# A decoder trunk in three-part float32 products: the order of seven products on PSUM accumulators, the place of a norm's scale, and the order of gates, tail and end of attention

## The chip, the cores and the metric

The kernel runs on one core of one Trainium2 chip. Its metric is the device time of one execution in microseconds (us). The engines are TensorE (PE in the profile), VectorE (DVE), ScalarE (ACT) and GpSimd (POOL); SyncE (SP) only issues transfers. Each engine works through its own list of instructions in order and waits for others by semaphores.

## What is computed

One layer of a decoder on 512 tokens of width 1024, in float32. x is the residual stream:

```
h = rmsnorm(x, g_mix);  proj = h @ w_in            # q, k, v of two attentions, two gates
y_a = stick_breaking_attention(...) @ w_up_a;  y_b = sliding_window_attention(...) @ w_up_b
x = x + (sigmoid(gate_a) * y_a + sigmoid(gate_b) * y_b) @ w_o
h = rmsnorm(x, g_mlp)
x = x + square(relu(h @ w_ff1)) @ w_ff2            # hidden width 4096
pe = p @ w_pe                                      # p: 512 x 256
x = x + pe * sigmoid(rmsnorm(x, g_pe) @ w_pg)
return rmsnorm(x, g_final)
```

rmsnorm multiplies by 1/sqrt(mean of squares + 1e-6) and by a weight g for each column.

## The kernel before

Each float32 operand of a product is split into a high part (a rounding to a shorter format, made by ACT) and a low part (the rest, made by DVE); `split` does this, and `mm3` makes three matrix products of the parts (high x high, low x high, high x low) on one PSUM bank. `unit` loads a block of 128 x 1024 weights by SP into a buffer wr and splits it into whi and wlo. PSUM has eight banks, named by tags: p (3), z (2), at (2), o (1).

The stages are: the first projections; sliding-window attention (`sliding`); values and, pair by pair of heads, `project` and `breaking` (stick-breaking attention, whose head h ends in a product `so` and whose pair ends in the operand oa, for the last pair oa3h and oa3l); gates ag and bg (`gates`, 24 matrix products each) and outputs ay and by (`outputs`, 12 each); merged gates times w_o (wo); the second norm and transposes to h2; the MLP; then the gate product pg, pe times its sigmoid, and the final norm.

The MLP's hidden columns are taken in four quarters q. A quarter has eight hidden blocks f (24 matrix products each, then relu and square into u). Its product with w_ff2 is done by a scheme of seven half-size products instead of eight (`products`): operands are sums and differences of quarters of u (s1, s2, s3, made by DVE) and of w_ff2. The sums of weights are made by transfers: SP loads a block into tx or t1, and POOL issues further loads that add to what is there. The seven products, p1 to p7, have 24 matrix products each and go to accumulators pa, pb, pc of two banks each; `onto` adds an accumulator to x2, the residual stream in SBUF. `products` is a generator; the loop over hidden blocks takes one step of the quarter before after each block, in the order p1, p7, p6, p2, p5, p4, p3, so that only the last quarter's seven stand without blocks between them. The first product is also kept in `both`, over all quarters, and added to three parts of x2 at the end.

The order within the engines is made by a scheduler from the order of the code, the free buffers and its own estimate; only the first stage has its ACT and DVE order by hand. In the second norm, r2 = 1/sqrt(mean + eps) is found by small DVE steps and x times r2 is written to xn; PE does `embed` (pe = p @ w_pe, both halves of 512 columns) meanwhile, then transposes xn. In the tail `injected` takes a bank of pg: sigmoid (ACT, L672), times pe and plus x2 (DVE, L673, L675), square with a sum over the row (ACT, L677), times g_final (POOL, L681). For each of the four row tiles t, `rsqrt` makes 1/sqrt by eight small steps (L119 to L130), both halves are scaled (L716 on DVE, L718 on ACT) and sent out (L719).

Of the kernel before, what the change touches and what calls it, by code (L numbers as in the profile page):

```python
# [17 lines left out]
P = 128  # L18
# [15 lines left out]
FOUR = ("p", "p", "z", "z")  # L34
# [8 lines left out]
def trunk(ctx, tc, xT_in, x_in, pT_in, w_in, w_up_a, w_up_b, w_o, w_ff1, w_ff2, w_pe, w_pg, g_final, pack, scratch, out):  # L43
# [12 lines left out]
    every = ["p", "p", "p", "z", "z", "at", "at", "o"]  # L56
# [371 lines left out]
    def gates(name, i):  # L428
        for m in (2 * i, 2 * i + 1):
            ps = bank(f"{name}g{m}")  # L430
            columns(ps, unit(w_in[(18 if name == "a" else 26) + m], P), h1)
            g = scaled(slot(f"{name}t{m}", "x" if name == "b" else "t"), ps, rb)
            nc.scalar.activation(g, g, AF.Sigmoid)
            gate[name, m] = g

    def outputs(name, i):
        w = unit((w_up_a if name == "a" else w_up_b)[i], 256)
        for j in range(2):
            m = 2 * i + j
            g = gate[name, m]  # L440
            ps = bank(f"{name}y{m}")
            columns(ps, w, oa if name == "a" else ob, j * P)
            nc.vector.tensor_tensor(g, g, ps, op=ALU.mult)
# [38 lines left out]
    def plain(name):  # L482
        return fpool.tile([P, U], F32, tag="raw", name=name, bufs=10)

    def factor(name):
        return [fpool.tile([P, U], F32R, tag=f"m{e}", name=f"m{e}{name}", bufs=3) for e in ("hi", "lo")]

    def half(name, tag, n):
        return fpool.tile([P, S], F32, tag=tag, name=name, bufs=n)
# [5 lines left out]
    phl = [b.rearrange("p (k c) -> p k c", k=2) for b in factor("pT")]  # L495
    split(*phl, pT)


    x2 = [[slot(f"x2_{t}{j}", "x") for j in range(2)] for t in range(NT)]
    ss = [small(f"ss2_{j}", 4) for j in range(2)]  # L500
    for j in range(2):
        for t in range(NT):
            nc.sync.dma_start(x2[t][j], x_in[t * P:(t + 1) * P, j * S:(j + 1) * S])
        ps = [bank(f"wo{j}_{t}", (FOUR, ("at", "at", "o", "p"))[j][t]) for t in range(NT)]
        for c in range(4):
            whi, wlo = unit(w_o[4 * j + c], S)
            for k in range(2):
                hi, lo = merged[2 * c + k]
                for t in range(NT):
                    cols = slice(t * P, (t + 1) * P)  # L510
                    mm3(ps[t], hi[:, cols], lo[:, cols], whi[:, k], wlo[:, k], c == 0 and k == 0, c == 3 and k == 1)
        for t in range(NT):
            nc.vector.tensor_tensor(x2[t][j], x2[t][j], ps[t], op=ALU.add)
            junk = half(f"junk{j}{t}", "e", 3)
            nc.scalar.activation(junk, x2[t][j], AF.Square, accum_out=ss[j][:, t:t + 1])
# [8 lines left out]
    pe = [[half(f"pe{t}{j}", "pe", 8) for j in range(2)] for t in range(NT)]  # L524

    def embed(j):
        whi, wlo = unit(w_pe[j], S)
        ps = [bank(f"pe{j}_{t}", ("p", "p", "z", "z" if j == 0 else "z")[t]) for t in range(NT)]
        for k in range(2):
            for t in range(NT):  # L530
                cols = slice(t * P, (t + 1) * P)
                mm3(ps[t], phl[0][:, k, cols], phl[1][:, k, cols], whi[:, k, :], wlo[:, k, :], k == 0, k == 1)
        for t in range(NT):
            nc.scalar.copy(pe[t][j], ps[t])

    embed(0)
    embed(1)

    h2 = [pair(f"h2_{k}", "h") for k in range(KD)]
    for k in range(KD):  # L540
        ps = bank(f"h2p{k}", every[k])
        for t in range(NT):
            nc.tensor.transpose(ps[:, t * P:(t + 1) * P], xn[t][:, k * P:(k + 1) * P], ident)
        split(*h2[k], ps, gcol(1, k))
# [3 lines left out]
    both = [half(f"both{t}", "e", 3) for t in range(2)]  # L548
    tt = nc.vector.tensor_tensor

    def products(q, ua, ub):
        a11, a21 = [ua[:, :, i * 256:(i + 1) * 256] for i in range(2)]
        a12, a22 = [ub[:, :, i * 256:(i + 1) * 256] for i in range(2)]
        b11, b21, b22, t1, tx = [[None] * 2 for _ in range(5)]

        def block(c, kh, jh):
            return w_ff2[((q * 2 + kh) * 2 + jh) * 2 + c]

        def load(name, c, kh, jh):
            b = plain(f"{name}_{q}{c}")  # L560
            nc.sync.dma_start(b, block(c, kh, jh))
            return b

        def more(t, kh, jh):
            for c in range(2):
                nc.gpsimd.dma_start(t[c], block(c, kh, jh), accum_op=ALU.add)  # L566

        for c in range(2):
            b11[c], tx[c], t1[c], b22[c] = load("b11", c, 0, 0), load("tx", c, 0, 1), load("t1", c, 0, 1), load("b22", c, 1, 1)
        more(tx, 1, 1)  # L570
        more(t1, 0, 0)

        def area(name, tags):
            return [bank(f"{name}{q}_{i}", tags[i]) for i in range(2)]

        def product(name, a, b, ps, start, stop, g=None):
            m = [x.rearrange("p (k c) -> p k c", k=4) for x in factor(f"{name}{q}")]
            split(*m, a, g)
            for c in range(2):
                count[0] += 1  # L580
                w = [wpool.tile([P, U], F32R, tag=f"w{e}", name=f"w{e}{count[0]}", bufs=3) for e in ("hi", "lo")]
                split(*w, b[c])
                whi, wlo = [x.rearrange("p (k c) -> p k c", k=2) for x in w]
                for k in range(2):
                    for i in range(2):
                        cols = slice(i * P, (i + 1) * P)
                        mm3(ps[i], m[0][:, 2 * c + k, cols], m[1][:, 2 * c + k, cols], whi[:, k], wlo[:, k],
                            start and c == 0 and k == 0, stop and c == 1 and k == 1, not start)
# [5 lines left out]
        def mix(name, x, y, op):  # L594
            s = fpool.tile([P, U], F32, tag="s", name=f"{name}_{q}", bufs=2).rearrange("p (k c) -> p k c", k=4)
            tt(s, x, y, op=op)
            return s

        pa, pc, pb = area("pa", ("z", "z")), area("pc", ("at", "at")), area("pb", ("o", "p"))
        product("p1", a11, b11, pa, True, True)  # L600
        yield
        product("p7", mix("s3", a11, a21, ALU.subtract), tx, pb, True, True)
        more(tx, 0, 0)
        for c in range(2):
            b21[c] = load("b21", c, 1, 0)
        for t in range(2):
            if q == 0:
                nc.scalar.copy(both[t], pa[t])
            else:
                tt(both[t], both[t], pa[t], op=ALU.add)  # L610
        yield
        s1 = mix("s1", a21, a22, ALU.subtract)
        s2 = mix("s2", s1, a11, ALU.subtract)
        product("p6", s2, tx, pc, True, True)
        more(tx, 1, 0)
        onto(pb, 1, 1)
        yield
        product("p2", a12, b21, pa, False, True)
        onto(pc, 1, 0)
        yield  # L620
        product("p5", s1, t1, pc, False, True, -1.0)
        onto(pa, 0, 0)
        yield
        nc.vector.scalar_tensor_tensor(s2, a12, -1.0, s2, op0=ALU.mult, op1=ALU.subtract)
        product("p4", a22, tx, pb, False, True)
        onto(pc, 1, 1)
        if q == 3:
            for i, j in ((0, 1), (1, 0), (1, 1)):
                onto(both, i, j)
        yield  # L630
        product("p3", s2, b22, pc, False, True)
        onto(pb, 1, 0)
# [3 lines left out]
    before = iter(())  # L636
    for q in range(4):
        uu = [big(f"u{q}{i}", i, F32).rearrange("p (k c) -> p k c", k=4) for i in range(2)]
        for m in range(8):
# [5 lines left out]
            next(before, None)  # L645
        before = products(q, *uu)
    for _ in before:
        pass

# [3 lines left out]
    h3 = [pair(f"h3_{k}", "h") for k in range(KD)]  # L653
    for k in range(KD):
# [135 lines left out]
```

## Time and profile before

| | us |
|---|---|
| median of 3 runs (752.1 to 753.82) | 752.29 |
| the profiled execution | 751.94 |
| its span, first to last instruction | 750.2 |
| PE busy | 727.5 |
| DVE busy | 503.8 |
| ACT busy | 370.8 |
| POOL busy | 66.8 |

The profile shows one execution. A busy time is the sum of an engine's instructions without overlaps. An idle time is put down to the instruction that ended last before the waiting one could start. The granted clock of PE is a share of full speed (2.4 GHz); 0.5 of it is the lower level of 1.2 GHz. The times of instructions that follow one another overlap a little, since an instruction's end is counted when its last result is written.

### The profile page before, as it was taken

The page shows a single profiled execution, that of the slowest core. Times are in us where ns is not written, and L with a number is a line of the kernel's source. Part 1 is how long each engine was busy: PE and PEld are TensorE (multiplying, and loading weights), DVE is VectorE, ACT ScalarE, POOL GpSimd, SP SyncE. Part 2 cuts the span into 40 slices and gives each one's busy share as a digit, 9 for nine tenths or more (in the row PEclk, how much of TensorE's full clock was granted, in tenths as well). Part 3 has the DMA queues.
Part 4 walks back from the last instruction along what each step waited for, and adds up shares of the span by engine and source line. Part 5 has one row for each costly group of instructions (what it writes and reads, how often), then busy time and mean ns, then how long its engine had stood idle before and what let it go on. Part 6 is the DMA issues. An engine that isn't in the chain of part 4 may idle for free.

```text
span 750.2 us, 9200 instructions
## 1 busy us (share of the span) xinstructions
PE 727.5 (97%) x3468; PEld 608.4 (81%) x3468; DVE 503.8 (67%) x734; ACT 370.8 (49%) x603; POOL 66.8 (9%) x88
## 2 busy tenths in 40 slices
PE   8999999999999899999999999999999999988993
PEld 7899888888888688888888888888888888867783
DVE  5595885998877476336446566576557675797576
ACT  7168978775444333338334344344434443456332
POOL 2010000211110000000000100010001100100042
PEclk9999999999999999999999999999999999999998
DMA  8331222132122053427934758477655777333002
GB/s 312 113 114 57 85 92 83 50 112 86 57 84 85 29 174 121 153 86 246 299 128 117 163 169 198 139 159 179 176 187 126 163 180 200 64 54 100 13 1 112
DMA packets 28043, 95.06 MB, mean 127 GB/s; under 512 B 3160, under 2 KB 3288, under 8 KB 28000
## 3 DMA queue, kind: packets, MB, share of 16 engines
q1 hardware_dynamic: 22320, 75.51, 29.8%
q0 software_dynamic: 4960, 17.84, 13.7%
q10 hardware_dynamic: 720, 1.13, 0.4%
q8 instruction: 27, 0.44, 0.2%
q14 instruction: 16, 0.13, 0.1%
HBM read 92.36 MB, written 2.11 MB: 126 GB/s over the span
## 4 chain that ended last, share of the span: by engine, by line
PE 84%; DVE 6%; issue 4%; ACT 3%; DMA 2%; POOL 0%; ACTq 0%; POOLq 0%; DVEq 0%
PE f L96 7%; PE f L98 7%; PE f L97 7%; PE pc L96 2%; PE pc L98 2%; PE pc L97 2%; PE bg L96 2%; PE bg L97 2%; PE bg L98 2%; PE ag L96 2%; PE ag L97 2%; PE ag L98 2%; PE wo L97 2%; PE wo L96 2%; PE wo L98 2%
## 5 line engine op out<-in xcount | busy, mean ns | idle before, releaser
L79 DVE TENSOR_TENSOR wlo<-wr,whi 128x1024 fp32r<-128x1024 f32 x88 | 107.5, 1223 | 116.0 <-ACT whi L78 115.5
L78 ACT CAST whi<-wr 128x1024 fp32r<-128x1024 f32 x88 | 92.4, 1052 | 177.0 <-PE f L97 80.8
L566 POOL DMA_DIRECT2D tx<-in_w_ff x24 | 20.8, 865 | 337.7 <-PE pe L98 124.8
L79 DVE TENSOR_TENSOR wlo<-b,whi 128x1024 fp32r<-128x1024 f32 x24 | 29.3, 1222 | 24.9 <-ACT whi L78 24.9
L78 ACT CAST whi<-b 128x1024 fp32r<-128x1024 f32 x24 | 25.2, 1052 | 34.2 <-PE f L97 12.2
L79 DVE TENSOR_TENSOR wlo<-tx,whi 128x1024 fp32r<-128x1024 f32 x24 | 29.3, 1221 | 12.9 <-ACT whi L78 12.8
L98 PE MATMUL pc<-whi,mlop 128*128 128x512 f32 x96 | 37.3, 391 | 0.0
L97 PE MATMUL pc<-wlo,mhip 128*128 128x512 f32 x96 | 37.3, 390 | 0.0
L96 PE MATMUL pc<-whi,mhip 128*128 128x512 f32 x96 | 36.4, 389 | 0.0
L78 ACT CAST whi<-tx 128x1024 fp32r<-128x1024 f32 x24 | 25.2, 1049 | 20.4 <-DMA tx<-in_w_ff 4.2
L397 DVE TENSOR_TENSOR_SCAN keep<-keep 128x128 f32<-128x128 f32 (+3 forms) x32 | 26.3, 860 | 3.8 <-POOL keep L392 1.9
L97 PE MATMUL pa<-wlo,mhip 128*128 128x512 f32 x64 | 25.6, 400 | 2.0 <-DVE wlo L79 2.0
L98 PE MATMUL pa<-whi,mlop 128*128 128x512 f32 x64 | 25.4, 397 | 0.0
L96 PE MATMUL pa<-whi,mhip 128*128 128x512 f32 x64 | 25.4, 402 | 0.0
L97 PE MATMUL pb<-wlo,mhip 128*128 128x512 f32 x64 | 25.0, 390 | 0.0
L98 PE MATMUL pb<-whi,mlop 128*128 128x512 f32 x64 | 24.9, 389 | 0.0
L97 PE MATMUL wo<-wlo,mg 128*128 128x512 f32 x64 | 24.9, 389 | 0.0
L96 PE MATMUL wo<-whi,mg 128*128 128x512 f32 x64 | 24.9, 389 | 0.0
L98 PE MATMUL wo<-whi,mg 128*128 128x512 f32 x64 | 24.7, 389 | 0.0
L96 PE MATMUL pb<-whi,mhip 128*128 128x512 f32 x64 | 23.9, 389 | 0.0
L644 DVE TENSOR_TENSOR u<-u,f 128x512 f32<-128x512 f32 x32 | 21.8, 680 | 0.0
L97 PEld LDWEIGHTS pc<-wlo,mhip 128*128 128x128 f32 x96 | 18.0, 188 | 4.0 <-DVE wlo L79 0.3
(986 smaller groups left out, 2163.3 us busy)
## 6 DMA issues: line engine op xcount, KB each, us to landing
wr<-in_w_in SPq DMA_DIRECT2D x34, 512.0 KB, 3.4
wr<-in_w_ff SPq DMA_DIRECT2D x32, 512.0 KB, 4.2
b<-in_w_ff SPq DMA_DIRECT2D x24, 512.0 KB, 4.2
tx<-in_w_ff POOLq DMA_DIRECT2D x24, 512.0 KB, 5.4
wr<-in_w_o SPq DMA_DIRECT2D x8, 512.0 KB, 3.4
tx<-in_w_ff SPq DMA_DIRECT2D x8, 512.0 KB, 3.3
t<-in_w_ff SPq DMA_DIRECT2D x8, 512.0 KB, 5.2
t<-in_w_ff POOLq DMA_DIRECT2D x8, 512.0 KB, 6.6
```

The costliest lines, as they stand in the source:

```text
L78: nc.scalar.copy(hi, src)
L79: nc.vector.tensor_tensor(lo, src, f32(hi), op=ALU.subtract)
L96: nc.tensor.matmul(ps, ahi, bhi, start=start, stop=False, skip_group_check=more)
L97: nc.tensor.matmul(ps, ahi, blo, start=False, stop=False, skip_group_check=more)
L98: nc.tensor.matmul(ps, alo, bhi, start=False, stop=stop, skip_group_check=more)
L397: nc.vector.tensor_tensor_scan(rev, rev, rev, 1.0, op0=ALU.mult, op1=ALU.min)
L566: nc.gpsimd.dma_start(t[c], block(c, kh, jh), accum_op=ALU.add)
L644: tt(u, u, ps, op=ALU.mult)
```

## The change

It does five things.

1. `gates("a", i)` is called for all four i before any `outputs("a", i)`; four of the gates get buffers of the tag qk, and two outputs go to banks of the tag z.
2. The second norm's r2 is not applied to x. h2 is made from x2, `turned` transposing four column blocks inside the second half of wo and four after `embed(0)`. Since relu and square of r2 times a number are r2 squared times those of the number, each product is multiplied by rr = 1/(mean + eps) when `onto` adds it to x2 (with -rr for the second column half), by one DVE step with a scalar. The small steps and the eight scalings of xn go.
3. The seven products take the order p1, p7, p6, p4, p5, p2, p3 on accumulators pc and pb (pa, for p2, takes pb's banks), each added to x2 when it is done; `both` goes. p1 and p7 are made after hidden blocks 5 and 6 of their own quarter, the other five after blocks 0 to 4 of the next. The weight sum for p4 now comes right after that for p6 in the same buffers tx (in the last quarter p6 has its own, ty). Buffers: eight instead of ten for loads, two instead of three for operands; weight halves of a product come from two pools.
4. Pe's second half, `embed(1)`, is made after the last hidden block, before the last quarter's p6. The first four blocks of h3 are transposed inside p3 (`first`), and the first quarter of pg comes ahead of the other four.
5. From there on ACT and DVE keep the order of the code (`manual_schedule`). The factor g_final is multiplied by DVE instead of POOL, for the second half within the last scaling; the square of a tile is taken after the sigmoid of the next one in the first half of pg, and right away in the second.

The diff, cut to its core:

```diff
+    for i in range(4):
+        gates("a", i)
...
-        if i == 0:
-            gates("a", 0)
-            gates("a", 1)
-        elif i > 1:
-            gates("a", i)
         outputs("a", i)
...
+    def turned(name, dst, i, k, tag):
+        ps = bank(f"{name}p{k}", tag)
+        for t in range(NT):
+            nc.tensor.transpose(ps[:, t * P:(t + 1) * P], x2[t][k // 4][:, k % 4 * P:(k % 4 + 1) * P], ident)
+        split(*dst[k], ps, gcol(i, k))
...
+            if j == 1 and c == 1:
+                for k in range(4):
+                    turned("h2", h2, 1, k, ("p", "p", "p", "z")[k])
...
-    r2 = rsqrt_mean("r2", ss[0], 4)
-    xn = [plain(f"xn{t}") for t in range(NT)]
-    for t in range(NT):
-        nc.scalar.mul(xn[t][:, :S], x2[t][0], r2[:, t:t + 1])
-        nc.vector.tensor_scalar(xn[t][:, S:], x2[t][1], r2[:, t:t + 1], None, op0=ALU.mult)
...
+    nc.vector.reciprocal(rr[0], ss[0])
+    nc.vector.tensor_scalar(rr[1], rr[0], -1.0, None, op0=ALU.mult)
...
         def onto(ps, i, j):
             for t in range(2):
-                tt(x2[2 * i + t][j], x2[2 * i + t][j], ps[t], op=ALU.subtract if j else ALU.add)
+                nc.vector.scalar_tensor_tensor(x2[2 * i + t][j], ps[t], rr[j][:, 2 * i + t:2 * i + t + 1],
+                                               x2[2 * i + t][j], op0=ALU.mult, op1=ALU.add)
...
+        product("p6", sums, ty, pc)
+        s1, s2 = ss
+        onto(pb, 1, 1)
+        if q < 3:
+            more(tx, 1, 0)
+        yield
+        product("p4", a22, tx, pb)
+        onto(pc, 1, 0)
...
+            if last and m < 5:
+                next(last)
+            if m in (3, 5, 6):
+                next(this)
...
+    with tc.manual_schedule(engines={mybir.EngineType.Activation, mybir.EngineType.DVE}):
+        emb = embed(1, ("o", "p", "p", "p"))
+        for step in (emb, emb, last, emb, last, last, last, last):
+            next(step)
...
+            if n == 1:
+                squared(t, 1, *made)
+                scaled_gf(t)
...
+            finish(t, v)
```

What the change does to the order is shown at three places. The first is PE at the end of attention: at and so are transposes and output of head 7, ay an output, ag a gate. Before:

```order
L409 MATMUL at7_1_2023<-ident_79,beta7_1981 128x128 x4
L98 MATMUL ay2_2646<-oa2h_1823,wlo36_2643 128x512
L416 MATMUL so7_2013<-aT7_0h_2015,va0_470 128x512
L409 MATMUL at7_2_2032<-ident_79,beta7_1981 128x128 x2
L417 MATMUL so7_2013<-aT7_0l_2016,va0_470 128x512
L416 MATMUL so7_2013<-aT7_1h_2024,va0_470 128x384
L417 MATMUL so7_2013<-aT7_1l_2025,va0_470 128x384
L416 MATMUL so7_2013<-aT7_2h_2033,va1_471 128x256
L417 MATMUL so7_2013<-aT7_2l_2034,va1_471 128x256
L416 MATMUL so7_2013<-aT7_1h_2024,va1_471 128x128
L417 MATMUL so7_2013<-aT7_1l_2025,va1_471 128x128
L96 MATMUL ay0_2606<-oa3h_2050,whi35_2602 128x512
```

After, the end of so7 on PE:

```order
L94 MATMUL ag7_2700<-h1_0h_111,whi38_2703 128x512
L414 MATMUL so7_2013<-aT7_2h_2033,va1_471 128x256
L95 MATMUL ag7_2700<-h1_0l_112,whi38_2703 128x512
L415 MATMUL so7_2013<-aT7_2l_2034,va1_471 128x256
L414 MATMUL so7_2013<-aT7_1h_2024,va1_471 128x128
L415 MATMUL so7_2013<-aT7_1l_2025,va1_471 128x128
L96 MATMUL ag7_2700<-h1_0h_111,wlo38_2704 128x512
```

The first use of oa3h stood right behind so7; it now stands behind the other 22 products of ag7 and nine of ay0. at7_1 now stands 26 products of ag5 and ag6 ahead of the first so7.

The second place is ACT at the start of pg. h3p is a bank of transposes, h3_0h the high part of the first h3 block, whi141 that of pg's first weight block, mhip33, whi139 and whi140 belong to p3, junc is a square. Before:

```order
L78 CAST whi140_5665<-b22_31_5386 128x1024
L78 CAST whi141_5804<-wr141_5802 128x1024
L663 ACTIVATE junc02_5765,ss3_0_5759<-x2_20_2914 128x512
L663 ACTIVATE junc03_5767,ss3_0_5759<-x2_30_2916 128x512
L78 CAST whi142_5834<-wr142_5832 128x1024
L78 CAST wpg0_5946<-wr145_5950 128x1024
L78 CAST whi143_5864<-wr143_5862 128x1024
L81 ACTIVATE h3_0h_5687<-h3p0_5703,pk_97 128x512
```

After:

```order
L76 CAST mhip33_5646<-s2_3_5491 128x1024
L76 CAST whi139_5650<-b22_30_5402 128x1024
L76 CAST whi140_5654<-b22_31_5403 128x1024
L79 ACTIVATE h3_0h_3324<-h3p0_5672,pk_97 128x512
L79 ACTIVATE h3_1h_3326<-h3p1_5679,pk_97 128x512
L76 CAST whi141_5688<-wr141_5686 128x1024
L79 ACTIVATE h3_2h_3328<-h3p2_5692,pk_97 128x512
L79 ACTIVATE h3_3h_3330<-h3p3_5699,pk_97 128x512
```

The splits of pg's weights stood ahead of the first h3 split, with squares between; now the first weight's split stands behind two h3 splits, and the squares come later.

The third place is ACT in the tail, from the sigmoid of the second half of row tile 0 (pgs0_1) on. Before:

```order
L672 ACTIVATE pgs0_1_5991<-pg1_00_5966,r3y_5780 128x512
L677 ACTIVATE pgs0_1_5991,ssd0_5794<-x2_01_2911 128x512
L718 ACTIVATE x2_01_2911<-x2_01_2911,r4_0y_6000 128x512
L672 ACTIVATE pgs1_1_6040<-pg1_10_6015,r3y_5780 128x512
L719 DMA out<-x2_01_2911 128x512
L677 ACTIVATE pgs1_1_6040,ssd1_5795<-x2_11_2913 128x512
L672 ACTIVATE pgs2_1_6089<-pg1_20_6064,r3y_5780 128x512
L677 ACTIVATE pgs2_1_6089,ssd2_5796<-x2_21_2915 128x512
L672 ACTIVATE pgs3_1_6138<-pg1_30_6113,r3y_5780 128x256
L718 ACTIVATE x2_11_2913<-x2_11_2913,r4_1y_6049 128x512
```

After:

```order
L725 ACTIVATE pgs0_1_5971<-pg1_00_5946,r3y_5887 128x512
L735 ACTIVATE pgs0_1_5971,ssd0_5921<-x2_01_2915 128x512
L752 ACTIVATE x2_00_2914<-x2_00_2914,r4_0y_5980 128x512
L755 DMA out<-x2_00_2914 128x512
L725 ACTIVATE pgs1_1_6020<-pg1_10_5995,r3y_5887 128x512
L735 ACTIVATE pgs1_1_6020,ssd1_5922<-x2_11_2917 128x512
L752 ACTIVATE x2_10_2916<-x2_10_2916,r4_1y_6029 128x512
```

The sigmoids of tiles 2 and 3 stood ahead of the scaling of tile 1; now each tile is scaled and sent before the next sigmoid.

## Rows read from the trace of the kernel before

**Rows 1.** Timeline of PE: start and duration in us, engine, line, operation, out<-in, count
```profile
638.43 0.39 PE L96 MATMUL f<-h_0h,whi 128*128 128x512 f32 x1
...
639.11 0.39 PE L96 MATMUL f<-h_1h,whi 128*128 128x512 f32 x1
...
687.01 3.00 PE L657 MATMUL h3p<-ident,x 128*128 128x128 f32 x26
...
737.46 0.28 PE L98 MATMUL pg<-wpg,h_7l 128*128 128x256 f32 x1
```

**Rows 2.** Stretches: length, busy us of PE, PEld, DVE, ACT, POOL; clock; DMA
```profile
500.00:525.00 25.00, 25.00 (x112) 20.71 (x111) 16.54 (x18) 11.01 (x12) 2.58 (x3) 1.00 0.74 178
252.00:262.00 10.00, 6.99 (x26) 4.94 (x26) 5.04 (x9) 4.16 (x7) 0.00 (x0) 0.83 0.01 2
258.00:262.00 4.00, 3.86 (x10) 3.05 (x11) 2.02 (x4) 1.03 (x2) 0.00 (x0) 0.57 0.02 4
...
664.00:668.00 4.00, 4.00 (x12) 3.08 (x12) 4.00 (x6) 1.01 (x1) 0.00 (x0) 0.57 0.01 4
690.00:696.00 6.00, 2.99 (x12) 1.85 (x12) 4.68 (x7) 6.00 (x13) 0.00 (x0) 1.00 0.58 178
```

**Rows 3.** What PE waited for: us in total, times, longest
```profile
PE ay L96 <- ACT oa3h L78: 2.0, 1, 2.0
PE pa L97 <- DVE wlo L79: 2.0, 1, 2.0
PE pg L96 <- DVE h_0l L82: 1.5, 1, 1.5
```

**Rows 4.** Timeline of DVE and ACT at the end of attention; brackets: idle before
```profile
252.77 0.68 DVE L420 TENSOR_TENSOR oa<-so,satmp 64x512 f32<-64x512 f32 x1 [5.33 <-ACT satmp L419]
...
257.47 0.62 ACT L78 CAST oa3h<-oa 128x512 fp32r<-128x512 f32 x1 [0.76 <-DVE oa L420]
```

**Rows 5.** Timeline of DVE and ACT, splits of weights and of h3
```profile
661.97 2.35 DVE L79 TENSOR_TENSOR wlo<-b,whi 128x1024 fp32r<-128x1024 f32 x2
...
690.75 0.74 DVE L82 SCALAR_TENSOR_TENSOR h_0l<-h3p,pk,h_0h 128x512 fp32r<-128x512 f32 x1
...
656.95 2.02 ACT L78 CAST whi<-b 128x1024 fp32r<-128x1024 f32 x2
...
689.29 0.68 ACT L81 ACTIVATE h_0h<-h3p,pk 128x512 fp32r<-128x512 f32 x1
```

**Rows 6.** Timeline of the tail, DVE, ACT and POOL
```profile
734.34 0.21 DVE L709 TENSOR_SCALAR v<-ssd,v 128x1 f32<-128x1 f32 x1 [0.79 <-ACT pgs L677]
...
742.20 0.41 DVE L673 TENSOR_TENSOR pgs<-pgs,pe 128x256 f32<-128x256 f32 x1
...
743.90 0.15 DVE L119 TENSOR_SCALAR r_3y<-ssd 128x1 int32<-128x1 int32 x1
744.09 0.66 DVE L114 SCALAR_TENSOR_TENSOR r_3w<-r_3y,ssd 128x1 f32<-128x1 f32 x1
...
745.16 0.22 DVE L114 SCALAR_TENSOR_TENSOR r_3w<-r_3y,ssd 128x1 f32<-128x1 f32 x1
...
731.43 0.67 ACT L672 ACTIVATE pgs<-pg,r3y 128x512 f32<-128x512 f32 x1
...
738.67 0.71 ACT L718 ACTIVATE x<-x,r_1y 128x512 f32<-128x512 f32 x1
...
739.79 0.47 ACT L672 ACTIVATE pgs<-pg,r3y 128x256 f32<-128x256 f32 x1 [0.42 <-ACT x L718]
...
746.11 0.72 ACT L718 ACTIVATE x<-x,r_3y 128x512 f32<-128x512 f32 x1 [2.61 <-DVE r_3y L130]
...
744.01 0.72 POOL L681 TENSOR_TENSOR x<-x,gf 128x256 f32<-128x256 f32 x1 [2.19 <-DVE ssd L679]
```

**Rows 7.** Tile tx: POOL's issues (ns min/median/max, first and last) and landings
```profile
L566 POOL DMA_DIRECT2D tx<-in_w_ff x24: 851/860/947, 352.2 to 658.9; - x24
...
DMA to landing us min/median/max: 3.2/5.4/11.5
```

More of the change, by code (lines that the diff above doesn't have):

```diff
@@ L440, in outputs @@
             g = gate[name, m]
[L441 removed]
+            ps = bank(f"{name}y{m}", "z" if name == "a" and m in (3, 4) else "p")
             columns(ps, w, oa if name == "a" else ob, j * P)
@@ L587, in product @@
                         mm3(ps[i], m[0][:, 2 * c + k, cols], m[1][:, 2 * c + k, cols], whi[:, k], wlo[:, k],
-                            start and c == 0 and k == 0, stop and c == 1 and k == 1, not start)
+                            start and c == 0 and k == 0, c == 1 and k == 1, not start)
+                if c == 0 and then:
+                    then()
         def onto(ps, i, j):
             for t in range(2):
-                tt(x2[2 * i + t][j], x2[2 * i + t][j], ps[t], op=ALU.subtract if j else ALU.add)
@@ L600, in products @@
-        product("p1", a11, b11, pa, True, True)
+        b11, tx = load("b11", 0, 0), load("tx", 0, 1)
+        more(tx, 1, 1)
         yield
-        product("p7", mix("s3", a11, a21, ALU.subtract), tx, pb, True, True)
-        more(tx, 0, 0)
[L604 to L610, printed above, removed]
-        yield
@@ L612, in products @@
[L612 to L615, printed above, removed]
+        pc, pb = area("pc", "at"), area("pb", "z")
+        product("p1", a11, b11, pc, True)
+        yield
+        product("p7", mix("s3", a11, a21), tx, pb, True)
+        onto(pc, 0, 0)
+        more(tx, 0, 0)
+        ty = tx
+        if q == 3:
+            more(tx, 1, 0)
+            ty = load("ty", 0, 1)
+            more(ty, 1, 1)
+            more(ty, 0, 0)
@@ L630, in products, with rest, first @@
-        yield
-        product("p3", s2, b22, pc, False, True)
-        onto(pb, 1, 0)
+        def rest():
+            onto(pa, 0, 0)
+            if q == 3:
+                first()
+        product("p3", s2, b22, pc, then=rest)
         onto(pc, 0, 1)
         yield
-    before = iter(())
+    h3 = [pair(f"h3_{k}", "h") for k in range(KD)]
+    wg = []
+    def first():
+        for k in range(4):
+            turned("h3", h3, 2, k, ("p", "p", "p", "o")[k])
+            if k % 2:
+                wg.append(unit(w_pg[k // 2], S))
@@ L637, in trunk @@
+    last = None
     for q in range(4):
         uu = [big(f"u{q}{i}", i, F32).rearrange("p (k c) -> p k c", k=4) for i in range(2)]
+        this = products(q, *uu)
         for m in range(8):
@@ L644, in trunk @@
             tt(u, u, ps, op=ALU.mult)
[L645 to L648, printed above, removed]
+            if last and m < 5:
+                next(last)
+            if m in (3, 5, 6):
+                next(this)
+        last = this
     gf = cpool.tile([P, D], F32, tag="vb", name="gf")
     nc.sync.dma_start(gf, bass.AP(g_final.tensor, g_final.offset, [[0, P], [1, D]]))
-    h3 = [pair(f"h3_{k}", "h") for k in range(KD)]
-    for k in range(KD):
-        ps = bank(f"h3p{k}", every[k])
-        for t in range(NT):
-            nc.tensor.transpose(ps[:, t * P:(t + 1) * P], x2[t][k // 4][:, k % 4 * P:(k % 4 + 1) * P], ident)
-        split(*h3[k], ps, gcol(2, k))
```

250 lines of the change are left out of this document (134 added, 116 removed).

## The prediction

> **What bounds the kernel now.** I first read the table of what TensorE (PE) waited for, then the busy time of short stretches around the waits it names, then the instructions there in order of time. Before and after hold the same number of PE instructions, matrix products and transposes of the same shapes, so the change can only touch the time in which PE stands still or runs at half clock, and what follows its last product. From row to row a product of 512 columns takes (639.11 - 638.43) / 3 = 0.2267 us, so a unit of 24 (one hidden block f, or one of the seven products, called p1 to p7) takes 5.44 us; 26 transposes take 3.00, 0.115 each; the last product starts at 737.46, in a run that steps by 0.12 [rows 1]. In the stretch where hidden blocks and products alternate PE is busy 25.00 of 25.00 us while VectorE (DVE) has 16.54 and ScalarE (ACT) 11.01 [rows 2]: nothing is to be had there. PE's losses sit in three places [rows 2, 3].
> A, end of attention: between 252 and 262 PE is busy 6.99 of 10.00 us, so 3.0 idle; the longest wait is 2.0 for oa3h. After it the granted clock is 0.57 from 258 to 262, the half level of 1.2 GHz in most of it, which costs 4 x 0.43 = 1.7. Sum 4.7.
> B, the products of the last quarter (q = 3), which have no hidden blocks left beside them: a wait of 2.0 for a weight split on DVE; then again clock 0.57 for 4 us, 1.7. Sum 3.7.
> C, start of the gate product pg: 2.99 busy of 6.00, so 3.0 idle, at full clock. ACT is busy all 6.00 us: squares and weight splits stand between the splits of h3 there.
> So 11.4 us can be had. The tail, from the last product (737.6) to the end of the span (750.2), is 12.6 more, and it is ACT and DVE alone.
>
> **The change part by part.**
> *End of attention (A).* The code now makes all eight gates ag before any output ay. Before, PE had one ay product between the last transposes of head 7 and its output so7, and none between so7 and the first use of oa3h. Now 22 products of ag7 and 9 of ay0 stand behind so7: 31 x 0.2267 = 7.0 us of cover. What has to pass under it is three steps, a copy, an add (0.68) and a cast (0.62), for which PE waited 2.0 us [rows 3, 4]. Earlier in the chain 24 and more products of ag5 and ag6 lie between at7 and so7. DVE was waiting for ACT 5.33 us ahead of the add [rows 4], so it is not the limit. The whole of A goes: -4.7. The eight ay in a row ask of DVE, for two of them, six steps of some 0.6 (0.68 less the overlap of steps in a row) and a weight split of 1.2 (2.35 for two in a row [rows 5]), 4.8 us against 5.44 of PE: hidden, by a little.
> *Second norm.* Eight scalings of x and a chain of small steps go; h2 is made from x itself and 1/(mean + eps) multiplies each sum when it is added to x. PE has no row of a wait in the old place, since pe covered it, so the removal is worth 0. Now half of the h2 transposes stand inside the wo product and pe of one half covers the rest: 5.44 us, and then 21 hidden products (4.8 us) that need only h2_0 to h2_3, against four splits of 0.68 on ACT and 0.74 on DVE, less 0.1 each where they follow one another [rows 5]. 0. The 56 added steps that scale are DVE steps with two tensors and a scalar; the nearest one takes 0.74 against 0.68 for the plain add [rows 4, 5]: 3.4 us of DVE time in all, in a stretch where DVE has 34% free [rows 2]. 0.
> *Seven products on two accumulators, fewer buffers.* Each sum is now added to x at once, and p6 and p4 stand side by side while p1 and p7 go under the hidden blocks of their own quarter. Two buffers for an operand instead of three: a product's split waits for the end of the product two before it. Between hidden blocks that is always over a whole block (5.44 us) early. 0, with a rival on the accumulating loads below.
> *Last quarter (B).* p1 and p7 are already done, and the other half of pe stands before p6. I laid the five last products out by hand, from the start of the last hidden block (t = 0) with 5.44 per unit, 0.96 for each further ACT cast of an operand or weight half and 1.14 for each further DVE step (two take 2.02 and 2.35, the first alone 1.05 and 1.22 [rows 5]). The low half of p6's operand is there at 11.8; PE comes to p6 at 10.9 and first needs it four products (0.9) later; the units end at 10.9 (pe), 16.4 (p6), 21.8 (p4), 27.2 (p5), 32.7 (p2). p5's last weight half is there at 21.7, p2's first at 25.7: both in time, p5's with little room. For p3 the adds after p5 end at 28.9 and its operand is mixed by 30.0, cast by 31.1; the weight is cast by 32.1 and its low half done at 33.5, which PE wants at 33.2: 0.3 lost. So B goes, -3.7, and +0.3 comes. If ACT or DVE is later than this by 1 us, p5 and p3 stand still for about as much.
> *Start of pg (C).* Four h3 now come from x's first half before p3 has been added to the second, and the squares are moved behind them. But in ACT's new order the split of the first pg weight stands behind h3_0 and h3_1, which wait for the transposes, though its data is there long before. Transposes of k = 0 and 1 end 0.9 us after p3, then 0.58 + 0.58 (0.68 less 0.1) + 1.05 on ACT with small hand-offs: the weight is there some 2.3 us later, while PE has only 1.0 us of other transposes left [rows 1, 5]. PE stands still for 1.35 and, four products (0.9) on, 0.35 more for the low half of that weight on DVE (1.22). After that the second half of the h3 splits is ahead. -3.0 and +1.7.
> *The tail.* On the same clock the second half of pg begins at 65.6 (seven units 38.1, 32 transposes 3.7, four units 21.8, 2.0 lost). PE begins the first three rows together (21 products of 512 and three of 256 columns, 5.1), then takes 17 for each of t = 0, 1, 2 and 45 of 256 columns for t = 3: they end at 74.6, 78.4, 82.3 and 87.7. The work behind each is in strict program order on ACT and DVE: sigmoid, two DVE steps, square, ten small DVE steps, scaling, the issue of the output, and only then the sigmoid of the next t. One round by the rows [rows 6]: sigmoid to the first small step, 734.34 - 731.43 = 2.9; that step 0.24; the inverse root from 743.90 to 746.11 = 2.2, less 0.44; scaling and issue to the next sigmoid, 739.79 - 738.67 = 1.1. Sum 6.0 us, while PE needs 3.9 per t: the round is the limit. Three rounds are 18.1, the last t with its two halves 4.8 (0.47, twice 1.3 as from 742.20 to 743.90 less the 0.4 of another step, 1.77), and from the last scaling to the end 750.2 - 746.11 = 4.1. That is 27.0 after 74.6, or 101.6; the last product ends at 87.7: 13.9 against 12.6 before, +1.3.
> The 0.44 is a choice. The second L114 of this chain takes 0.22, the first 0.66, and it ends with an L681 of GpSimd (POOL) that runs beside it, here 744.01 to 744.73 [rows 6]. The change takes L681 away, so I take 0.22 for both. If the length belonged to the step itself, four times 0.44 would come back, 1.8. The Trainium skill, page "SBUF — State Buffer", section "Who interferes with whom", says that a DVE step with two SBUF inputs and a POOL step that reads SBUF share a read port, and the one that comes second waits until the other is done. By that rule the result is the forecast's; the trace agrees (744.75 against 744.73).
>
> **Sum.** -4.7 - 3.7 - 3.0 + 0.3 + 1.7 + 1.3 = -8.1. The profiled execution took 751.94 us with a span of 750.2; 751.94 - 8.1 = 743.8. It lies 0.35 below the median of 752.29, so on the median's footing I forecast 744.2 us.
>
> **Rivals.**
> R1, half clock after the new gap: 1.35 and 0.35 us of idle before pg bring another stretch at 0.57, +1.7: 745.9. For it: a wait of 2.0 did so twice. Against it: the wait of 1.5 in C did not [rows 2, 3].
> R2, the long small step stays: 744.2 + 1.8 = 746.0, as above.
> R3, the attention chain is slow by itself and PE, with gates ahead of it, still waits for it: A stays, 748.9. Against it: between heads 0 and 6 the same chain passes under gates and outputs without a row in PE's waits.
> R4, slower than before: the accumulating loads. For p7, p6 and p4 one buffer tx is loaded, split, added to by a POOL load and split again. Before, five other units lay between p6 and p4; now p4 follows p6 at once, and its split stands on ACT ahead of the operand of p6. From the release of tx by p6's split there are p7 and three hidden blocks, 21.8 us, of which some 6 go to the splits and casts queued there: landing may take about 16 us. The landings are 3.2 to 11.5, median 5.4 [rows 7]. At 18 us each of the first three quarters would stop PE for 2 us and bring 1.7 of half clock: 3 x 3.7 = 11.1, 755.3. One rule of the Trainium skill speaks for it: "SBUF — State Buffer", section "SBUF: two separate sides", says that a load issued by POOL can starve while certain DVE steps hold the shared port. The trace gives no sign of it: 24 issues last 851 to 947 ns beside a busy DVE [rows 7].
> R5, the tail is hidden better than I think, since casts overlap or issues are short: no loss there, and PE's gap in C half as long: 744.2 - 1.3 - 0.7 = 742.2.
>
> **How the numbers follow.** Forecast 0.58 (743 to 745.5), R1 0.12, R2 0.08, R3 0.08, R4 0.06, R5 0.08. From 742 to 748.5 lie the forecast, R1, R2, their sum (747.7) and R5; R3 and R4, 0.14, and some unforeseen small waits are left out. Less than 0.3% (2.3 us), which measurement can't tell from no change, would need more than 750.0: R4 and R3 with anything added. Faster 0.87, same 0.07, slower 0.06.
>
> **What would show it.** In the profile after: no PE row for oa3h or so7 and clock 1.00 around 255; no PE wait between hidden blocks; a PE wait of some 1.4 us for the cast of the first pg weight, at full clock; sigmoids of the tail 6.0 us apart and 14 us from the last product to the end; L114 at 0.22 throughout. The forecast is wrong if waits for tx or for x stand in PE's table before the last quarter, if p3 or p5 waits for over 1 us, or if the sigmoids come 3.9 apart, which would mean that PE and not the round sets the tail.

## The result, and the profile after

The changed kernel takes 743.09 us in the median of 4 runs (742.94 to 744.36), the one before 752.98 us in runs on the same chip: ratio 0.9872, 95% interval 0.9854 to 0.9891. The profiled execution took 743.24 us with a span of 741.5, against 751.94 and 750.2: 8.7 less, where the forecast said 8.1 less. The forecast time was 744.2 us. The medians differ by 9.9, since the one before lies 1.0 above its profiled execution and the one after does not.

The table of what TensorE (PE) waited for, after: us in total, times, longest. It stands against [rows 3].

```profile
PE pg L94 <- ACT whi L76: 1.3, 1, 1.3
PE warm L144 <- DVE ones L138: 1.1, 1, 1.1
PE kb L95 <- DVE h_0l L80: 0.8, 1, 0.8
PE kb L94 <- ACT h_0h L79: 0.4, 1, 0.4
```

The waits for oa3h and for the weight of pa are gone, and with them every wait between the head of the kernel and pg; there the wait for h_0l is replaced by one for the first weight of pg. The chain to oa3h now runs beside products; PE's timeline from so7's last product to the first use of oa3h, then ACT's cast of it (ns min/median/max, first and last start):

```profile
265.42 0.28 PE L415 MATMUL so<-aT_1l,va 128*128 128x128 f32 x1
...
272.64 0.39 PE L94 MATMUL ay<-oa3h,whi 128*128 128x512 f32 x1
```

```profile
L76 ACT CAST oa3h<-oa x1: 622/622/622, 267.8 to 267.8; 128x512 fp32r<-128x512 f32 x1
```

Stretches after, columns as in [rows 2]:

```profile
500.00:525.00 25.00, 25.00 (x112) 20.71 (x111) 17.89 (x20) 10.98 (x13) 3.47 (x4) 1.00 0.87 224
252.00:262.00 10.00, 10.00 (x51) 8.41 (x50) 6.10 (x8) 5.05 (x8) 0.00 (x0) 1.00 0.20 70
258.00:262.00 4.00, 4.00 (x21) 3.33 (x20) 2.34 (x3) 1.96 (x3) 0.00 (x0) 1.00 0.13 40
649.00:655.00 6.00, 6.00 (x28) 4.69 (x27) 5.42 (x6) 5.00 (x8) 0.00 (x0) 1.00 0.00 1
676.00:682.00 6.00, 4.63 (x28) 3.58 (x27) 3.21 (x5) 4.04 (x6) 0.00 (x0) 1.00 0.00 0
```

PE is full and at clock 1.00 at the end of attention and in the last quarter (649 to 655). The one gap left is at pg (676 to 682), at full clock.

Where the 8.7 us come from is read best from the starts of five products that exist in both kernels: the first product of all, the first of wo, the first hidden block f, the last one, and the last product of pg. Timeline of PE before (the last two are in [rows 1]), then after:

```profile
6.42 0.50 PE L96 MATMUL kb<-h_0h,whi 128*128 128x512 f32 x1 [0.21 <-ACT h_0h L81]
...
297.31 0.39 PE L96 MATMUL wo<-whi,mg 128*128 128x512 f32 x1
...
355.42 0.50 PE L96 MATMUL f<-h_0h,whi 128*128 128x512 f32 x1
```

```profile
7.03 0.51 PE L94 MATMUL kb<-h_0h,whi 128*128 128x512 f32 x1 [0.41 <-ACT h_0h L79]
...
292.36 0.39 PE L94 MATMUL wo<-whi,mg 128*128 128x512 f32 x1
...
344.76 0.47 PE L94 MATMUL f<-h_0h,whi 128*128 128x512 f32 x1
...
638.64 0.39 PE L94 MATMUL f<-h_0h,whi 128*128 128x512 f32 x1
...
726.23 0.28 PE L96 MATMUL pg<-wpg,h_7l 128*128 128x256 f32 x1
```

| stretch | before | after | work moved into it | gain or loss | forecast |
|---|---|---|---|---|---|
| head | 6.42 | 7.03 | 0 | +0.6 | 0 |
| to wo (A) | 290.89 | 285.33 | 0 | -5.6 | -4.7 |
| wo, second norm | 58.11 | 52.40 | -5.44 (half of pe) | -0.3 | 0 |
| hidden blocks | 283.01 | 293.88 | +10.88 (two products) | 0.0 | 0 |
| last quarter, pg (B, C) | 99.03 | 87.59 | -5.44 | -6.0 | -4.7 |
| tail, from the last product's start | 12.74 | 15.27 | 0 | +2.5 | +1.3 |
| sum | | | | -8.7 | -8.1 |

The head has the same code in both; in the twelve profiled executions of kernels with that head its first product starts between 6.38 and 7.03, so its 0.6 is not put down to the change. The tail after, timeline of ACT: sigmoids (L725) are 6.05 apart, and the last scaling (L752) starts 4.84 ahead of the end of the span.

```profile
713.51 0.69 ACT L725 ACTIVATE pgs<-pg,r3y 128x512 f32<-128x512 f32 x1 [2.31 <-PE pg L96]
...
718.39 0.72 ACT L752 ACTIVATE x<-x,r_0y 128x512 f32<-128x512 f32 x1 [1.99 <-DVE r_0y L128]
719.15 0.37 ACTq L755 DMA_DIRECT2D out<-x  x1
719.56 0.69 ACT L725 ACTIVATE pgs<-pg,r3y 128x512 f32<-128x512 f32 x1 [0.45 <-ACT x L752]
...
731.67 0.84 ACT L725 ACTIVATE pgs<-pg,r3y 128x256 f32<-128x256 f32 x2 [0.45 <-ACT x L752]
736.66 0.72 ACT L752 ACTIVATE x<-x,r_3y 128x512 f32<-128x512 f32 x1 [4.15 <-DVE r_3y L128]
```

### The profile page after: what moved, and what is told of

The parts are those of the page before. It is cut to its first block, busy times and chain, and to the rows that moved or that the text cites. A ratio compares the mean times of both kernels' runs of the same rounds, so it can differ in the third digit from the quotient of the medians.

```text
span 741.5 us, 9197 instructions
## 1 busy us (share of the span) xinstructions
PE 722.8 (97%) x3468; PEld 606.5 (82%) x3468; DVE 499.6 (67%) x722; ACT 366.5 (49%) x598; POOL 58.4 (8%) x83
## 4 chain that ended last, share of the span: by engine, by line
PE 95%; DVE 2%; ACT 1%; DMA 1%; issue 0%; ACTq 0%; DVEq 0%
PE f L95 8%; PE f L94 8%; PE f L96 8%; PE pc L96 4%; PE pc L95 4%; PE pc L94 4%; PE bg L94 2%; PE bg L96 2%; PE bg L95 2%; PE ag L96 2%; PE ag L94 2%; PE ag L95 2%; PE wo L96 2%; PE wo L94 2%; PE pb L94 2%; PE pb L95 2%
## 5 line engine op out<-in xcount | busy, mean ns | idle before, releaser
L95 PE MATMUL pc<-wlo,mhip 128*128 128x512 f32 x128 | 49.8, 389 | 0.0
L96 PE MATMUL pc<-whi,mlop 128*128 128x512 f32 x128 | 49.3, 390 | 0.0
L94 PE MATMUL pc<-whi,mhip 128*128 128x512 f32 x128 | 49.2, 389 | 0.0
L76 ACT CAST whi<-tx 128x1024 fp32r<-128x1024 f32 x22 | 23.1, 1056 | 40.0 <-PE f L95 22.0
L77 DVE TENSOR_TENSOR wlo<-tx,whi 128x1024 fp32r<-128x1024 f32 x22 | 26.8, 1223 | 20.5 <-ACT whi L76 20.4
L96 PEld LDWEIGHTS pc<-whi,mlop 128*128 128x128 f32 x128 | 23.9, 188 | 5.3 <-DVE mlop L77 0.3
L94 PEld LDWEIGHTS pc<-whi,mhip 128*128 128x128 f32 x128 | 24.0, 188 | 5.0
L95 PEld LDWEIGHTS pc<-wlo,mhip 128*128 128x128 f32 x128 | 24.0, 188 | 5.0
L678 DVE TENSOR_TENSOR u<-u,f 128x512 f32<-128x512 f32 x32 | 21.8, 680 | 5.3 <-ACT u L677 5.3
L95 PE MATMUL wo<-wlo,mg 128*128 128x512 f32 x64 | 24.9, 389 | 0.0
L95 PE MATMUL pb<-wlo,mhip 128*128 128x512 f32 x64 | 24.9, 389 | 0.0
L599 DVE SCALAR_TENSOR_TENSOR x<-pc,rr,x 128x512 f32<-128x512 f32 x32 | 22.5, 744 | 0.4 <-PE pc L96 0.4
```

The source lines that it names most:

```text
L76: nc.scalar.copy(hi, src)
L77: nc.vector.tensor_tensor(lo, src, f32(hi), op=ALU.subtract)
L94: nc.tensor.matmul(ps, ahi, bhi, start=start, stop=False, skip_group_check=more)
L95: nc.tensor.matmul(ps, ahi, blo, start=False, stop=False, skip_group_check=more)
L96: nc.tensor.matmul(ps, alo, bhi, start=False, stop=stop, skip_group_check=more)
L599: nc.vector.scalar_tensor_tensor(x2[2 * i + t][j], ps[t], rr[j][:, 2 * i + t:2 * i + t + 1], x2[2 * i + t][j], op0=ALU.mult, op1=ALU.add)
```

## Experiments

**The gates alone, in the kernel before.** Their buffers are those of the change.

```diff
+    for i in range(4):
+        gates("a", i)
...
-        if i == 0:
-            gates("a", 0)
-            gates("a", 1)
-        elif i > 1:
-            gates("a", i)
```

> The kernel before with the first part of the change alone: all eight gates ag ahead of the outputs ay. My theory (7.0 us of products cover the chain to oa3h, and the half clock behind the wait goes too): 4.7 us less, from 752.3 to about 747.6, no wait for oa3h and clock 1.00 from 258 to 262. Counted from the start of one matmul to the start of another, the stretch is worth more than the idle rows show, 5.5, so 746.8 would not surprise. Rival (the chain is slow by itself and TensorE waits for it whatever stands ahead): no change, a wait of about 2 for oa3h in another place. Rival (the time comes back in a later stage, since the products there wait for something else): the first products of wo start 5 us earlier but the span is the same.

Measured: 748.28 against 753.40, ratio 0.993 (0.9908 to 0.9951), 5.1 less. There is no wait for oa3h any more. Stretches of this kernel, columns as above:

```profile
8.00:12.00 4.00, 3.95 (x10) 3.07 (x11) 3.84 (x6) 3.61 (x6) 0.00 (x0) 0.58 1.06 398
252.00:262.00 10.00, 10.00 (x52) 8.41 (x51) 6.08 (x8) 5.21 (x8) 0.00 (x0) 1.00 0.18 54
...
692.00:696.00 4.00, 4.00 (x14) 3.16 (x13) 4.00 (x10) 3.60 (x6) 0.00 (x0) 0.66 0.01 2
```

A is a gain of its own that no later stage gives back, by the medians. The profiled execution shows less, a span of 748.2 against 750.2, and the first and the last row say why: it ran part of the head at 0.58 and the start of pg at 0.66, where the profiled execution of before had 1.00 with the same code and, at pg, the same waits. To wo it takes 286.56 against 290.89, 4.3 less, and from the last f to the last product 100.92 against 99.03, 1.9 more; the stretches between are unchanged.

**The tail: next sigmoid ahead of this scaling.**

```diff
+        nxt = begun(*todo[0])
...
-            finish(t, v)
+            if u + 1 < len(todo):
+                nxt = begun(*todo[u + 1])
+            if i == n - 1:
+                finish(t, v)
```

Here `begun` makes a tile's products and its sigmoid; the rest of `injected`, the square and the small steps follow as before.

> The kernel after, with the tail's order changed on ScalarE: the sigmoid of the next row tile stands ahead of the scaling and sending of this one. My theory (the closed round sigmoid, two steps, square, ten small steps, scaling, output issue, sigmoid sets the tail): sigmoids then come about 4.9 apart, which is VectorE's own work of a round (714.23 to 719.14 in the kernel after), instead of 6.05; three rounds less 1.15 each, 3.4 us less, span 741.5 to about 738. Rival (TensorE sets the tail): no change. Rival (outputs and their transfers set it): no change either, but with sigmoids closer together.

Measured: 739.39 us, ratio 0.9817 (0.98 to 0.9835), span 737.6. From the last product's start to the end it is 11.87 against 15.27: the 3.4 expected. ACT's scalings (L753 here) are now 4.83 apart, VectorE's (DVE's) own round:

```profile
717.89 0.73 ACT L753 ACTIVATE x<-x,r_0y 128x512 f32<-128x512 f32 x1 [0.34 <-DVE r_0y L128]
...
722.72 0.73 ACT L753 ACTIVATE x<-x,r_1y 128x512 f32<-128x512 f32 x1 [1.38 <-DVE r_1y L128]
...
727.55 0.72 ACT L753 ACTIVATE x<-x,r_2y 128x512 f32<-128x512 f32 x1 [1.63 <-DVE r_2y L128]
```

So the closed round set the end of the changed kernel, and neither PE nor the outputs.

**The first weight of pg ahead of the h3 splits.**

```diff
     def first():
+        wg.append(unit(w_pg[0], S))
         for k in range(4):
             turned("h3", h3, 2, k, ("p", "p", "p", "o")[k])
-            if k % 2:
-                wg.append(unit(w_pg[k // 2], S))
+        wg.append(unit(w_pg[1], S))
```

> The kernel after, with the split of the first weight block of the gate product ahead of the h3 splits on ScalarE and VectorE. My theory (its data is there long before, and it only stands in the wrong place): TensorE's wait of 1.3 for the cast and the 0.35 for its low half go, and nothing else is late: 1.7 us less, span 741.5 to 739.8. Rival (the h3 splits are the limit at this place): TensorE waits for h_0h or h_0l instead, about the same 1.3, no change. Rival (the weight's buffer comes free late, so that the cast now holds up the h3 splits behind it): slower by up to 2.

Measured: 742.36 us, ratio 0.9857 (0.9838 to 0.9877), span 741.1. PE's wait is gone, and from the last f to the last product it is 86.13 against 87.59: 1.5 of the 1.7. The span shows 0.4 only, since this execution had the head at 0.57 (to wo 286.67 against 285.33, 1.3 more). Two rows of ACT's timeline show the order: the cast now ends 5.75 us before the first h3 split can start.

```profile
671.98 1.04 ACT L76 CAST whi<-wr 128x1024 fp32r<-128x1024 f32 x1
678.77 0.69 ACT L79 ACTIVATE h_0h<-h3p,pk 128x512 fp32r<-128x512 f32 x1 [5.75 <-PE h3p L516]
```

**Both.**

> The kernel after with both edits, the weight split first and the sigmoid of the next tile ahead. The two places lie one behind the other and share no resource at their limit, so the gains should add: 1.7 and 3.4, span 741.5 to about 736.4. Rival (the tail is limited by VectorE, which is busy without a break from 701 on, so that what TensorE gains ahead of it is lost there): the weight split's 1.7 vanishes and the span is that of the tail edit alone, about 738.

Measured: 738.15 us, ratio 0.9805 (0.9785 to 0.9824), span 736.1. Against the tail edit alone 1.2 in the median and 1.5 in the span: the gains add, and this is the fastest version, 4.9 below the changed kernel's median. Of the 1.5, 0.24 lies in the head (first product at 6.38 against 6.62); from the last f to the end it is 1.3, and the weight split alone gave 1.3 there too. DVE's tail starts when PE delivers, so it moves with it.

**Pe's second half back in its old place.**

```diff
+    for _ in embed(1, ("p", "p", "p", "z")):
+        pass
...
-        emb = embed(1, ("o", "p", "p", "p"))
-        for step in (emb, emb, last, emb, last, last, last, last):
+        for step in (last, last, last, last, last):
             next(step)
```

> The kernel after, with pe's second half made right behind its first half, ahead of the hidden blocks, as before, and not ahead of the last quarter's p6. My theory (these 5.44 us of products are what covers the making of p6's operand): in the kernel after the operand's high half is there at about 649.2 and TensorE would come to p6 at 644.1, so it stands still for 5.1 us, and half clock may follow (up to 1.7): 5.1 to 6.8 us more, span 741.5 to 746.6 or 748.3. Since ScalarE is rid of 2.0 us of copies, what follows p6 is not later. Rival (the new order of the seven products is what removes the wait, and the place of pe is of no weight): no change.

Measured: 750.40 us, ratio 0.9957 (0.9942 to 0.9972), span 748.7, 7.2 more. Its PE waits and two stretches:

```profile
PE pc L94 <- ACT mhip L76: 5.0, 1, 5.0
```

```profile
652.00:656.00 4.00, 1.43 (x3) 1.16 (x4) 2.85 (x4) 2.53 (x3) 0.00 (x0) 0.56 0.00 0
656.00:660.00 4.00, 4.00 (x12) 3.17 (x11) 4.00 (x5) 1.36 (x2) 0.00 (x0) 0.59 0.01 2
```

5.0 of it is idle, and most of the other 2.2 is what follows at the half level of 1.2 GHz. The new order of the products without this cover would have kept B's loss and more; it is pe that carries it.

**g_final by GpSimd (POOL) again, in the new order.**

```diff
-                    nc.vector.scalar_tensor_tensor(dst, dst, r4[:, 0:1], gf[:, S:], op0=ALU.mult, op1=ALU.mult)
+                    nc.vector.tensor_scalar(dst, dst, r4[:, 0:1], None, op0=ALU.mult)
...
                 squared(t, 1, *made)
                 scaled_gf(t)
+                nc.gpsimd.tensor_tensor(made[1], made[1], gf[:, S:], op=ALU.mult)
...
```

> The kernel after, with g_final multiplied into the second half of each row tile by GpSimd behind the square, as in the kernel before, instead of by VectorE within the scaling; the order on ScalarE and VectorE is that of the kernel after. My theory (the small step L112 is long only where a GpSimd step runs beside it, and ends with it): the first L112 of each round goes from 0.22 to some 0.9 where the GpSimd step has 512 columns and to 0.66 where it has 256, each round grows by that, 3 x 0.7 + 0.44 = 2.5 us more; the two halves of an output are again issued some 0.3 apart, and if that is why the end came 3.4 us behind the last scaling before and 4.1 after, 0.7 comes back: sum 1.8 more, span about 743.3. Rival (the long step was not caused by GpSimd): L112 stays at 0.22, rounds stay 6.05 apart.

Measured: 746.15 us, ratio 0.9898 (0.9884 to 0.9913), span 743.7; from the last product's start to the end 17.77 against 15.27, 2.5 more. Timeline of the first and last of the long L112 steps, one more step with two inputs, and the POOL steps beside them:

```profile
716.58 0.92 DVE L112 SCALAR_TENSOR_TENSOR r_0w<-r_0y,v 128x1 f32<-128x1 f32 x1
...
735.66 0.83 DVE L728 TENSOR_TENSOR x<-x,pgs 128x256 f32<-128x256 f32 x1
...
737.24 0.66 DVE L112 SCALAR_TENSOR_TENSOR r_3w<-r_3y,ssd 128x1 f32<-128x1 f32 x1
...
716.19 1.28 POOL L772 TENSOR_TENSOR x<-x,gf 128x512 f32<-128x512 f32 x1 [78.43 <-ACT pgs L735]
...
735.37 0.84 POOL L768 TENSOR_TENSOR x<-x,gf 128x256 f32<-128x256 f32 x1 [4.46 <-DVE ssd L730]
...
737.16 0.72 POOL L778 TENSOR_TENSOR x<-x,gf 128x256 f32<-128x256 f32 x1 [0.96 <-DVE ssd L730]
```

The DVE step ends at 717.50 where POOL's ends at 717.47, and at 737.90 where POOL's ends at 737.88; without POOL the same steps took 0.22. Rounds are 6.7 apart. The rule cited in the prediction from the Trainium skill ("SBUF — State Buffer", "Who interferes with whom") holds here, 0.92 against 0.22 us. The last tile lost 0.84, where 0.44 was expected: besides L112, the add L728, which also has two inputs, took 0.83 beside POOL's L768, where the one before it took 0.42. The end gave back 0.34 instead of 0.7.

**56 plain adds.**

```diff
-                nc.vector.scalar_tensor_tensor(x2[2 * i + t][j], ps[t], rr[j][:, 2 * i + t:2 * i + t + 1],
-                                               x2[2 * i + t][j], op0=ALU.mult, op1=ALU.add)
+                tt(x2[2 * i + t][j], x2[2 * i + t][j], ps[t], op=ALU.subtract if j else ALU.add)
```

> The kernel after, with the 56 steps that add an accumulator to x made as plain adds and subtractions, without the factor 1/(mean + eps), which so is left out of the computation. My theory: the factor costs VectorE 0.06 us a step, 3.4 us in all, all of it beside TensorE's work: no change in the span (within 0.3 us). Rival (VectorE is at its limit in the last quarter or the tail, and the steps there are on the path): up to 14 steps x 0.06 = 0.8 us less.

Measured: 742.76 us, ratio 0.9857 (0.9842 to 0.9872), span 741.1. Its PE times from product to product are those of the changed kernel within 0.1; the scale costs nothing.

**Longer sums in tx.** Three runs repeat an accumulating load in the first three quarters: for both sums, for p4's alone, for p6's alone.

```diff
-        more(tx, 0, 0)
+        for _ in range(2 if q < 3 else 1):
+            more(tx, 0, 0)
...
-            more(tx, 1, 0)
+            for _ in range(2):
+                more(tx, 1, 0)
```

> The kernel after, with one further accumulating load for each sum that p6 and p4 take from tx in the first three quarters (the block is added twice, so the sums are others than wanted): each of these sums takes twice as long to land, 10.8 us instead of 5.4 in the median. My estimate of the room on record is about 16 us, and p4's sum starts later by what p6's split loses: the room is just used up. I expect 0 to 1 us more for a quarter, 0 to 3 in all. Rival (the room is much smaller than I thought, and the changed kernel only just escapes): 5 us or more for each quarter, 15 and more in all, with TensorE waits for the cast of tx. Rival (the room is far larger): no change and no wait.

Measured for both: 775.58 us, ratio 1.0304 (1.0277 to 1.0332), span 770.8, 29 more. My estimate was wrong and the first rival right in size. What PE waited for is not the cast of tx itself but what stands behind it on ACT:

```profile
PE pc L94 <- ACT mhip L76: 10.1, 3, 4.4
PE f L94 <- ACT whi L76: 6.9, 2, 3.8
```

ACT's timeline in the first quarter, in the changed kernel (with PE's first product of p6) and then in this one:

```profile
404.70 1.05 ACT L76 CAST whi<-tx 128x1024 fp32r<-128x1024 f32 x1 [3.89 <-PE f L95]
405.65 0.59 ACT L677 ACTIVATE u<-f 128x512 f32<-128x512 f32 x1
406.14 1.04 ACT L76 CAST mhip<-s 128x1024 fp32r<-128x1024 f32 x1
...
410.16 0.39 PE L94 MATMUL pc<-whi,mhip 128*128 128x512 f32 x1
```

```profile
412.01 1.04 ACT L76 CAST whi<-tx 128x1024 fp32r<-128x1024 f32 x1 [9.96 <-DMA tx<-in_w_ff]
412.96 0.59 ACT L679 ACTIVATE u<-f 128x512 f32<-128x512 f32 x1
413.45 1.03 ACT L76 CAST mhip<-s 128x1024 fp32r<-128x1024 f32 x1
```

The cast for p4 stands on ACT ahead of a relu and of p6's operand; when its data is late, both are. PE came to p6 at 410.16 in the changed kernel, 3.0 us after that operand was there.

> The kernel after, with one further accumulating load for p4's sum alone, in the first three quarters (that sum is another than wanted). What the run with both sums doubled showed: in the first quarter the load for p4's first block is issued at 394.0, and its cast, which ScalarE reaches at 404.7 in the kernel after, stands ahead of a relu and of the cast of p6's operand; TensorE wants that operand 3.0 us later than it is there, so the room from issue to landing is about 13.7 us, and not 16 as I had it on record. Theory 1 (this one block is the tight place): two loads one behind the other took 17.1 us there, so nearly the whole loss of that run (29 us) comes back, 20 to 30 us more than 743. Theory 2 (only both sums together, the second starting late because of the first, use the room up): no change.

Measured for p4's sum alone: 750.54 us over runs from 746.61 to 756.66, ratio 0.9969 (0.9937 to 1.0001). PE's waits in an execution of 756.66:

```profile
PE pc L94 <- ACT mhip L76: 7.2, 3, 3.8
```

> The kernel after, with one further accumulating load for p6's sum alone, in the first three quarters (that sum is another than wanted). Theory 1 (p4's first block is the tight place, and p6's casts were not late in the run with both sums doubled: 391.35 against 391.32): no change, within 1 us of the kernel after. Theory 2 (p6's sum, doubled, is what made p4's late): a good part of the 29 us comes back.

Measured for p6's alone: 743.00 us, ratio 0.9869 (0.985 to 0.9888): no change. So p4's sum is the tight place, as Theory 1 had it, but doubled alone it costs some 7 us in the medians and not 20 to 30, where both cost 32. Longer landings alone do not explain that: the median of POOL's loads of tx is 5.5 in the changed kernel, 7.0 with p4's, 7.4 with both, and 7.8 with p6's, which costs nothing. The delays roughly add. Counted from the second quarter's first cast of tx, the first cast for p4 comes 21.0 later in the changed kernel, 24.9 with p4's, 27.7 with p6's and 33.0 with both. With both, it holds up the weight cast of the next hidden block, and that is the wait of 6.9 above, in the second and third quarters; in the other two runs PE never waits there. Why the runs with p4's alone spread over 10 us was not settled; the profiled one is the slowest of its nine, 13.5 above the changed kernel.

No run takes C's part by itself (four h3 transposes inside p3, the squares moved behind the splits): that this is what shortened the gap at pg is argued from the rows and from the run with the weight first.

## Why the prediction was right, point by point

- **A.** Right in mechanism: the first use of oa3h now stands at 272.64, 7.2 us behind so7's last product (7.0 was said), and oa3h is there at 268.4. The term was too small: -4.7 against -5.6, and -5.1 for this part alone. It was summed from idle rows and clock rows. The profile draws a product 0.39 long where the next can start 0.2267 later, so the first 0.16 of a wait is not counted as idle, and a shorter wait not at all; the products beside a wait were also some 0.1 slower each. Starts of products, less their count times 0.2267, hold all of it.
- **Second norm.** Forecast 0, measured -0.3; the 56 scaled adds cost nothing, as said.
- **Seven products.** No loss in the hidden stretch: 293.88 against 293.76 for 54 units of 5.44. R4 did not happen, but it was nearer than its text says. Its stretch from the release of tx to PE's use was counted wrong: p6's split frees the block when p7 is at its end (393.64 and 393.84), so that from the load's issue at 394.0 to p6 at 410.16 there are three hidden blocks, 16.2 us, and not p7 and three, 21.8. From the start of p4's cast to the end of that of p6's operand it is 2.5, where some 6 were taken off. That leaves 13.7, not 16, and the two errors partly offset. With p4's sum doubled the second landing came 17.5 after the first issue and PE waited 3.8, which is the difference. The price of 3.7 a quarter fits p4's sum alone (2.5 in the medians, 4.5 in the profiled execution); both sums doubled cost 29.3 / 3 = 9.8. What was late was the landing of two loads one behind the other: issues on POOL stayed at 0.86 us in the median, 1.21 at most, so no sign of the rule on a starving issue, cited beside R4 from the Trainium skill ("SBUF — State Buffer", "SBUF: two separate sides"), shows here.
- **B and C.** -4.7 said, -6.0 measured. Of the 99.03 us before, 8.1 were lost by the count of products (90.92), where idle and clock rows gave 6.7: the same fault as in A. The small items were near: p3 lost 0.06 instead of 0.3, p6 0.2 instead of 0; PE waited 1.31 for the cast of pg's first weight (1.35 said) and lost 0.34 at its low half (0.35 said), at full clock.
- **Tail.** +1.3 said, +2.5 measured. The rounds were right (three of 6.05, 18.1 said), and L112 took 0.22 throughout. The mis-sized term is the end: 4.84 from the last scaling's start, not 4.1. It has two parts. From that start to the landing of the last output it is 3.54, against 3.22 before: the two halves of the last output were issued 0.2 apart before (746.64 and 746.86) and halves landed in 2.2 in the median; after, 0.03 apart, in 2.7. The one pair that was issued 0.03 apart before (743.49 and 743.52) took 2.5 and 2.7. From the last landing to the end of the span it is 1.33 against 0.90: SP's queue ends with a row of waits for semaphores, 0.06 apart (the trace has them, the timeline leaves them out). Before, one of them stood behind the last landing; after, eight do. In the run with POOL the halves were again 0.2 apart and landed in 2.3, and the first part was 3.27; but seven waits still stood behind the last landing, 1.27, so only 0.34 of the 0.74 came back. The last tile took 4.99 (4.8), and from the first sigmoid to the end of PE's last product it was 12.84 (13.1), which also lengthens the tail.

```profile
DMA to landing us min/median/max: 2.0/2.2/2.7
```

```profile
DMA to landing us min/median/max: 2.6/2.7/2.9
```

(Outputs, before and after.) The terms were too small on either side: 2.4 more gain in A, B, C and the norm, 1.2 more loss in the tail and 0.6 in the head. They nearly met, which is luck: the sum came out better than its parts. R1 did not show in the profile after, but the run with the gates alone shows that the same waits at pg are followed by clock 0.66 in one execution and 1.00 in another, so its chance is one for each execution. R2, R3 and R5 fell: L112 is short, oa3h is covered, and rounds are 6.05 apart.

## What to carry to other kernels

Sum a stage's loss from the starts of two instructions that both kernels have, less the count of instructions times the step; idle rows hold only the part that outlasts a modelled end. Where an order is written by hand, look for an instruction that waits for the end of a chain while the start of the next chain stands behind it: here a scaling ahead of a sigmoid cost 3.4 us and a cast behind two splits 1.5. The room of a transfer is counted from the moment its buffer is freed to the first work behind its reader in the reader's queue, not to the reader's own use.

## What the hardware showed that I had not expected

Executions of the same code differ in where the half clock falls: at 8 to 12 us the granted clock was 0.57 and 0.58 in two of the twelve profiled executions and 1.00 in the others, worth 1.3 us. Two accumulating loads on one block, one behind the other, took 17.2 us with both sums doubled and 17.5 with p4's alone, where the median of one was 5.5. The loss grew from some 7 us to 32 in the medians when a second pair was added that by itself cost nothing. SP's row of semaphore waits at the end of the program cost 0.4 us more where eight of them, and not one, stood behind the last landing.
